# A hybrid attention block: where X's transposes, the first unit's round trip and the prelude's column sums stand

## The chip, the core and the metric

The kernel runs on one core of a Trainium2 chip. TensorE (PE) multiplies, VectorE (DVE), ScalarE (ACT) and GpSimd (POOL) work on elements, SyncE (SP) issues nearly all transfers. PE writes its results into PSUM, from where DVE and ACT fetch them. The metric is device microseconds of one execution, smaller is better.

## What is computed

One layer on 1024 tokens of width 1024. A vector c gives six modulation vectors. The normalized input, scaled and shifted by two of them, is u. From u come a softmax attention with a forget gate (8 heads of 64), an RWKV-7 time mix (8 heads of 64) and two sigmoid gates; their gated sum goes through w_o, and a gated feed-forward network with a short convolution follows.

```python
mod = silu(c) @ w_mod + b_mod                    # six parts of 1024
u = rms_norm(x, ln1_g) * (1 + scale1) + shift1
p_fox, p_rwkv, p_gate = split(u @ w_in)
o_fox  = softmax attention with forget gate (p_fox) @ fox_w_out
o_rwkv = rwkv7_time_mix(p_rwkv) @ rwkv_w_out
h = x + gate1 * ((sigmoid(p_gate[0]) * o_fox + sigmoid(p_gate[1]) * o_rwkv) @ w_o)
u2 = rms_norm(h, ln2_g) * (1 + scale2) + shift2
h = h + gate2 * ((silu(conv(u2 @ w_up_a)) * (u2 @ w_up_b)) @ w_down)
out = rms_norm(h, final_g)
```

The time mix is a recurrence over tokens; its state is updated with a decay, a rank-one removal and a rank-one addition per token.

## The kernel before

All large products run as three products of split operands (high times high, high times low, low times high). So each weight block is loaded as `raw`, copied to `hi` (ACT) and subtracted to `lo` (DVE) in `load_w`, and one column block of 128 for 1024 tokens is 48 products of 128x512, 24 for each half of the tokens.

**Prelude** (order on PE, SP, DVE and ACT as written). x is loaded in eight tiles (`xt`), squared, normalized and transposed by PE into `uf` (`turn`). The two modulation vectors come from `mod_load(i, ...)`, which loads eight weight tiles `wm`, `mod_add`, which adds them on DVE into `acc` with the weights `sc`, and `mod_sum`, in which PE sums `acc` over its 128 partitions column by column into `mps` and DVE adds the bias into `m1` (m in the trace) and forms `A1` (A). Part 1 (scale) is done first, then part 0 (shift). `warm` issues products that nobody reads. `u_steps` then goes through the eight tiles of each half of the tokens: uf is scaled and shifted, `u_hi` is a rounded copy, `u_lo` the rest. Behind each tile `low_part` issues four products into the four PSUM tiles `low`, two column blocks at a time.

**LoRA and RWKV stage.** PE's order comes from a planner, `Weave`: each chain is a Python generator that yields the time in planned nanoseconds after which it wants to go on, and until then the planner lays products of a queue of filler (q, k, r, v columns, gates) into PE's order. DVE, ACT, POOL and SP are ordered by the framework's scheduler from the program order and the dependencies. The time mix works in eight units (p, hf): four pairs of heads, two halves of the tokens, 8 chunks of 64 tokens each. `pre(k, p, hf)` prepares a unit: decays (`cum`, `el`, `en`), keys (`kr`, `bk`), queries (`ar`), products of them whose masked copies are E (four `tt` with the mask on DVE), and the inverse of a 32x32 triangular block: E goes by DMA to a scratch `sm`, back as M32, is inverted in 31 steps of two DVE operations (`t`, `E32`) and goes by DMA over `se` to TT. This is the round trip, for which `ready` is set: planned time plus 46000 in the first unit, 38500 in the others. `main(k, p, hf)` then transposes part of TT on DVE into X (two operations, one for each head), issues the products xi with X, then zi, uw, mz, and the chain of eight chunk states S; S waits on DVE for the product sp and the next products wait for S. A head normalization with y, mu and va ends the unit. The X transposes carry an order dependence on the last S issued so far (`marks["S"]`).

**Attention and later.** The gates that the units have not used as filler are woven into the attention as `rk_ps` products (`late_gate`), with their gs and gm on ACT and DVE. The attention itself is a chain per tile: lg (PE), nm (DVE), P (ACT, DVE), tp (PE), th (ACT), tl (DVE), ov (PE), o (ACT, DVE). Then come the branch products br, w_o and the feed-forward part.

Of the kernel before, what the change touches and what calls it, by code (L numbers as in the profile page):

```python
# [9 lines left out]
F32 = mybir.dt.float32  # L10
# [5 lines left out]
D = 1024  # L16
# [115 lines left out]
def hybrid_block(ctx: ExitStack, tc: tile.TileContext, a, out):  # L132
# [122 lines left out]
    def load_w(src, name, pool=None, n=1024, scale=None, tags=("whi", "wlo"), bufs=2):  # L255
# [14 lines left out]
        else:  # L270
            nc.scalar.copy(hi, raw)  # L271
# [73 lines left out]
    with ExitStack() as es:  # L345
# [66 lines left out]
        with tc.tile_pool(name="st", bufs=1) as st, tc.tile_pool(name="stp", bufs=2, space=PS) as stp, \  # L412
# [42 lines left out]
            def mod_sum(i, acc):  # L455
                for j0 in (0, 4):
                    ps = stp.tile([128, 4], F32, tag="mp", name=f"mps{i}{j0}")
                    for j in range(4):
                        c0 = (j0 + j) * 128
                        mm(ps[:, j : j + 1], acc[:, c0 : c0 + 128], ones[:, 0:1], start=True, stop=True)  # L460
                    tt(m1[:, i * 8 + j0 : i * 8 + j0 + 4], ps, V("b_mod", i * 8 + j0, 4), op=ALU.add)
                    if i == 1:
                        stt(A1[:, j0 : j0 + 4], m1[:, 8 + j0 : 12 + j0], 1.0, V("ln1_g", j0, 4), op0=ALU.add, op1=ALU.mult)
# [7 lines left out]
            def u_steps(half):  # L471

                cs = slice(half * NH, half * NH + NH)
                for kt in range(KT + 1):
                    if kt < KT:
                        x = uf[half][:, kt, :]
                        ts(x, x, A1[:, kt : kt + 1], m1[:, kt : kt + 1], op0=ALU.mult, op1=ALU.add)
                        nc.scalar.copy(u_hi[:, kt, cs], x)
# [33 lines left out]
            m = [mod_load(1, ("mw",)), None]  # L512
# [8 lines left out]
            m[1] = mod_load(0, ("xt", "mw"))  # L521
# [7 lines left out]
            nc.sync.dma_start(cst2, a["cst"][:, NC1:])  # L529
            for i in (1, 0):  # L530
# [292 lines left out]
        def main(k, p, hf):  # L823
# [9 lines left out]
            for h in range(2):  # L833
                i = nc.vector.transpose(X[B0[h], :, :], TT[B0[h], :, 0:32])
                if "S" in marks:
                    tc.add_manual_dep(i.ins, marks["S"].ins.name, NOSYNC)
# [1147 lines left out]
```

## Time and profile before

| | us |
|---|---|
| median of 3 runs | 1684.34 (1683.34 to 1690.74) |
| profiled execution | 1691.77 |
| its span, first to last instruction | 1690.0 |
| PE busy | 1645.9 |
| DVE busy | 1217.6 |
| ACT busy | 809.7 |
| POOL busy | 125.6 |

A row of a timeline gives start, duration, engine, line, operation, out<-in, count, and in brackets the idle time of the engine before it with what ended it. A row of the stretches gives the stretch and its length, then for each engine its busy time and in brackets the number of its instructions, then the granted clock of PE (1.00 is full), the share of DMA and GB/s. Products that follow each other overlap, so their step from start to start is shorter than their duration.

### The profile page before, as it was taken

The page shows a single profiled execution, that of the slowest core. Times are in us where ns is not written, and L with a number is a line of the kernel's source. Part 1 is how long each engine was busy: PE and PEld are TensorE (multiplying, and loading weights), DVE is VectorE, ACT ScalarE, POOL GpSimd, SP SyncE. Part 2 cuts the span into 40 slices and gives each one's busy share as a digit, 9 for nine tenths or more (in the row PEclk, how much of TensorE's full clock was granted, in tenths as well). Part 3 has the DMA queues.
Part 4 walks back from the last instruction along what each step waited for, and adds up shares of the span by engine and source line. Part 5 has one row for each costly group of instructions (what it writes and reads, how often), then busy time and mean ns, then how long its engine had stood idle before and what let it go on. Part 6 is the DMA issues. An engine that isn't in the chain of part 4 may idle for free.

```text
span 1690.0 us, 26279 instructions
## 1 busy us (share of the span) xinstructions
PE 1645.9 (97%) x9886; PEld 1353.3 (80%) x9886; DVE 1217.6 (72%) x2402; ACT 809.7 (48%) x1482; POOL 125.6 (7%) x150
## 2 busy tenths in 40 slices
PE   7999999999999999999999999999999999999998
PEld 7777777787877777888878888888888888888886
DVE  4786787678776625888768545897777777786677
ACT  5563334343454456667632233654444444454455
POOL 0011011111111002121022000000000000000000
PEclk9999999999999999999999999999999999999999
DMA  8487643434332226444187521133332333484463
GB/s 330 149 316 232 176 125 106 119 100 115 102 110 81 92 70 178 131 127 112 40 308 263 207 83 42 50 107 123 108 106 94 101 111 106 171 284 146 129 212 112
DMA packets 120975, 239.87 MB, mean 142 GB/s; under 512 B 39888, under 2 KB 48336, under 8 KB 120848
## 3 DMA queue, kind: packets, MB, share of 16 engines
q1 hardware_dynamic: 112896, 220.94, 40.1%
q0 software_dynamic: 7952, 17.25, 3.8%
q8 instruction: 78, 1.28, 0.3%
q14 instruction: 49, 0.40, 0.1%
HBM read 172.59 MB, written 65.54 MB: 141 GB/s over the span
## 4 chain that ended last, share of the span: by engine, by line
PE 77%; DVE 10%; DMA 6%; ACT 3%; issue 2%; SPq 2%; DVEq 0%; POOL 0%; ACTq 0%; POOLq 0%
PE X L140 13%; PE D L140 12%; PE Y L140 6%; PE wo L140 5%; PE gt L140 5%; PE ps_rkv L140 5%; PE br L140 5%; PE W L140 3%; PE rk_ps L140 3%; PE qk L140 3%; PE lg L140 2%; PE v L140 2%; PE ov L140 2%; PE sp L140 2%; PE tp L144 2%
## 5 line engine op out<-in xcount | busy, mean ns | idle before, releaser
L140 PE MATMUL D<-op,op 128*128 128x512 f32 x924 | 209.8, 389 | 0.0
L140 PEld LDWEIGHTS D<-op,op 128*128 128x128 f32 x924 | 173.3, 188 | 36.3 <-DVE op L1247 0.3
L140 PE MATMUL X<-T_m,S 128*128 128x512 f32 x440 | 107.3, 390 | 0.1
L140 PEld LDWEIGHTS X<-T_m,S 128*128 128x128 f32 x440 | 82.5, 188 | 18.2 <-ACT T_m L1672 0.6
L1246 ACT CAST op<-g 128x512 fp32r<-128x512 f32 x77 | 47.8, 621 | 72.9 <-PE D L140 48.0
L1247 DVE TENSOR_TENSOR op<-g,op 128x512 fp32r<-128x512 f32 x77 | 53.0, 689 | 41.0 <-ACT op L1246 40.8
L777 DVE TENSOR_TENSOR t<-E,M 128x60 f32<-128x60 f32 (+24 forms) x248 | 57.4, 232 | 32.6 <-DMA M<-sm 27.3
L1483 DVE SCALAR_TENSOR_TENSOR c<-ab,vec,c 128x512 f32<-128x512 f32 x88 | 65.9, 750 | 19.5 <-ACT c L1486 18.0
L273 DVE TENSOR_TENSOR lo_in<-raw_in,hi_in 128x512 fp32r<-128x512 f32 x84 | 56.5, 707 | 23.0 <-PE gt L140 12.1
L1447 DVE TENSOR_TENSOR S<-ur,S 128x512 fp32r<-128x512 f32 x66 | 45.5, 691 | 35.6 <-ACT S L1443 35.4
L1443 ACT CAST S<-ur 128x512 fp32r<-128x512 f32 x66 | 41.0, 622 | 55.6 <-DVE ur L1436 30.6
L271 ACT CAST hi_in<-raw_in 128x1024 fp32r<-128x1024 f32 x42 | 43.9, 1048 | 47.5 <-PE ps_rkv L140 18.9
L1447 DVE TENSOR_TENSOR A<-ur,A 128x512 fp32r<-128x512 f32 x64 | 44.1, 689 | 30.9 <-ACT A L1443 30.7
L140 PE MATMUL Y<-T_h,A 128*128 128x512 f32 x264 | 63.5, 389 | 0.0
L140 PE MATMUL Y<-T_h,S 128*128 128x512 f32 x264 | 63.3, 389 | 0.0
L1049 ACT ACTIVATE P<-lg,nm 128x896 f32<-128x896 f32 (+3 forms) x64 | 47.5, 743 | 30.0 <-DVE nm L1045 21.7
L140 PE MATMUL X<-B_b,A 128*128 128x512 f32 x252 | 60.8, 390 | 0.0
L140 PE MATMUL W<-B_f,A 128*128 128x512 f32 x252 | 60.6, 389 | 0.0
L140 PEld LDWEIGHTS Y<-T_h,A 128*128 128x128 f32 x264 | 49.6, 188 | 10.4
L140 PEld LDWEIGHTS Y<-T_h,S 128*128 128x128 f32 x264 | 49.6, 188 | 10.3
L779 DVE TENSOR_TENSOR E<-E,t 128x60 f32<-128x60 f32 (+24 forms) x248 | 53.2, 214 | 5.8
L1443 ACT CAST A<-ur 128x512 fp32r<-128x512 f32 x64 | 39.9, 623 | 34.2 <-PE X L140 33.6
(475 smaller groups left out, 4161.8 us busy)
## 6 DMA issues: line engine op xcount, KB each, us to landing
raw_in<-in_w_in SPq DMA_DIRECT2D x50, 512.0 KB, 3.8
wm<-in_w_mod SPq DMA_DIRECT2D x48, 512.0 KB, 7.1
ur<-in_w_up SPq DMA_DIRECT2D x44, 512.0 KB, 4.1
g<-d_g SPq DMA_DIRECT2D x35, 512.0 KB, 4.1
d_g<-gs SPq DMA_DIRECT2D x44, 256.0 KB, 2.0
d_g<-c SPq DMA_DIRECT2D x33, 256.0 KB, 4.5
d_st<-qh SPq DMA_DIRECT2D x64, 128.0 KB, 2.4
stA<-d_st POOLq DMA_DIRECT2D x8, 1024.0 KB, 6.3
```

Source lines behind the costliest of these rows:

```text
L140: nc.tensor.matmul(o, lhsT, rhs, start=start, stop=stop, skip_group_check=more)
L144: nc.tensor.transpose(o, i, eye)
L271: nc.scalar.copy(hi, raw)
L273: nc.vector.tensor_tensor(lo[:, c : c + NH], raw[:, c : c + NH], f32(hi[:, c : c + NH]), op=ALU.subtract)
L777: tt(tv, E32[:, 0:J, s : s + 1].to_broadcast([128, J, W]), M32[:, s : s + 1, s + 1 : 32].to_broadcast([128, J, W]), op=ALU.mult)
L779: tt(E32[:, 0:J, s + 1 : 32], E32[:, 0:J, s + 1 : 32], tv, op=ALU.add)
L1049: nc.scalar.activation(e[:, 0:n], lg[:, 0:n], AF.Exp, bias=nm[:, 0:1], accum_out=nm[:, 1:2])
L1246: nc.scalar.copy(hi, src)
L1247: tt(lo, src, f32(hi), op=ALU.subtract)
L1443: nc.scalar.copy(hi, src)
L1447: tt(lo, src, f32(hi), op=ALU.subtract)
L1483: stt(c, ab[:, x + hf * NH : x + hf * NH + NH], V("conv_w", 22 * x + i), c, op0=ALU.mult, op1=ALU.add)
```

## The change

In the prelude, part 1's eight column sums follow its `acc` at once and 43 warm products come behind them. DVE goes on with part 0; part 1's m and A are made behind the fifth addition of part 0. Part 0's column sums are made tile by tile in `u_steps`: columns 0, 1, 2 to 3, 4 to 7 ahead of tiles 0, 1, 2 and 4. Every second uf is scaled on ACT. The weight tiles get five buffers in place of four, and part 0's `acc` takes one of the x tiles' eight. The first copies of `load_w` come behind the last `u_hi` on ACT. In the time mix, the first unit's `ready` is 49500 in place of 46000; X's transposes are issued 2500 planned ns ahead of xi, where that is still to come, and in any case 2500 lie between them; and they are ordered behind the last mask E issued so far, besides the last S.

```diff
         else:
-            nc.scalar.copy(hi, raw)
+            i = nc.scalar.copy(hi, raw)
+            if "u" in marks:
+                tc.add_manual_dep(i.ins, marks.pop("u").ins.name, NOSYNC)
...
             def mod_load(i, tags):
-                ws = [st.tile([128, D], F32, tag=tags[kt % len(tags)], name=f"wm{i}{kt}", bufs={"mw": 4, "xt": 8}[tags[kt % len(tags)]])
-                      for kt in range(KT)]
-                for kt, w in enumerate(ws):
-                    nc.sync.dma_start(w, a["w_mod"][kt * 128 : kt * 128 + 128, i * D : i * D + D])
-                return ws, st.tile([128, D], F32, name=f"acc{i}")
+                ws = []
+                for kt in range(KT):
+                    tag = tags[kt % len(tags)]
+                    ws.append(st.tile([128, D], F32, tag=tag, name=f"wm{i}{kt}", bufs={"mw": 5, "xt": 8}[tag]))
+                    nc.sync.dma_start(ws[-1], a["w_mod"][kt * 128 : kt * 128 + 128, i * D : i * D + D])
+                return ws
...
-            def mod_sum(i, acc):
-                for j0 in (0, 4):
-                    ps = stp.tile([128, 4], F32, tag="mp", name=f"mps{i}{j0}")
-                    for j in range(4):
-                        c0 = (j0 + j) * 128
-                        mm(ps[:, j : j + 1], acc[:, c0 : c0 + 128], ones[:, 0:1], start=True, stop=True)
-                    tt(m1[:, i * 8 + j0 : i * 8 + j0 + 4], ps, V("b_mod", i * 8 + j0, 4), op=ALU.add)
-                    if i == 1:
-                        stt(A1[:, j0 : j0 + 4], m1[:, 8 + j0 : 12 + j0], 1.0, V("ln1_g", j0, 4), op0=ALU.add, op1=ALU.mult)
+            def mod_sum(i, acc, ps, j0, j1):
+                for j in range(j0, j1):
+                    mm(ps[:, j : j + 1], acc[:, j * 128 : j * 128 + 128], ones[:, 0:1], start=True, stop=True)
+
+            def mod_out(i, ps, j0, j1):
+                c = slice(i * 8 + j0, i * 8 + j1)
+                tt(m1[:, c], ps[:, j0:j1], V("b_mod", i * 8 + j0, j1 - j0), op=ALU.add)
+                if i == 1:
+                    stt(A1[:, j0:j1], m1[:, c], 1.0, V("ln1_g", j0, j1 - j0), op0=ALU.add, op1=ALU.mult)
...
                 for kt in range(KT + 1):
+                    if half == 0 and kt in (0, 1, 2, 4):
+                        ks = kt, max(kt + 1, 2 * kt)
+                        mod_sum(0, acc[0], mps[0], *ks)
+                        mod_out(0, mps[0], *ks)
                     if kt < KT:
                         x = uf[half][:, kt, :]
-                        ts(x, x, A1[:, kt : kt + 1], m1[:, kt : kt + 1], op0=ALU.mult, op1=ALU.add)
-                        nc.scalar.copy(u_hi[:, kt, cs], x)
+                        if kt % 2:
+                            nc.scalar.activation(x, x, AF.Identity, scale=A1[:, kt : kt + 1], bias=m1[:, kt : kt + 1])
+                        else:
+                            ts(x, x, A1[:, kt : kt + 1], m1[:, kt : kt + 1], op0=ALU.mult, op1=ALU.add)
+                        marks["u"] = nc.scalar.copy(u_hi[:, kt, cs], x)
...
-            m[1] = mod_load(0, ("xt", "mw"))
+            acc[0] = st.tile([128, D], F32, tag="xt", name="acc0", bufs=8)
+            ws[0] = mod_load(0, ("xt", "mw"))
...
             for i in (1, 0):
                 for kt in range(KT):
-                    mod_add(kt, *m[1 - i])
-                mod_sum(i, m[1 - i][1])
-                warm((6, 40)[i])
+                    mod_add(kt, ws[i], acc[i])
+                    if i == 0 and kt == 4:
+                        mod_out(1, mps[1], 0, KT)
+                if i == 1:
+                    mod_sum(1, acc[1], mps[1], 0, KT)
+                    warm(43)
...
-                    tt(E[:, c0 : c0 + 4, h, 0:2, :].rearrange("p c a s -> p c (a s)"), hx(ps[h], 128),
+                    marks["E"] = tt(E[:, c0 : c0 + 4, h, 0:2, :].rearrange("p c a s -> p c (a s)"), hx(ps[h], 128),
...
-            ready = weave.now + (46000 if k == 0 else 38500)
+            ready = weave.now + (49500 if k == 0 else 38500)
...
+            yield max(0, o["ready"] - weave.now - 2500)
             for h in range(2):
                 i = nc.vector.transpose(X[B0[h], :, :], TT[B0[h], :, 0:32])
-                if "S" in marks:
-                    tc.add_manual_dep(i.ins, marks["S"].ins.name, NOSYNC)
-            yield max(0, o["ready"] - weave.now)
+                for x in ("S", "E"):
+                    if x in marks:
+                        tc.add_manual_dep(i.ins, marks[x].ins.name, NOSYNC)
+            yield 2500
```

What this does to the order is shown at three places. First DVE in the prelude, from the last addition of part 0 to the sixth u tile (mps are the column sums in PSUM). Before:

```order
L453 SCALAR_TENSOR_TENSOR acc_334<-wm_325,sc,acc_334 128x1024
L461 TENSOR_TENSOR m_103<-mps_420,vec 128x4
L461 TENSOR_TENSOR m_103<-mps_426,vec 128x4
L477 TENSOR_SCALAR uf_172<-uf_172,A_102,m_103 128x512 x2
L481 TENSOR_TENSOR u_lo<-uf_172,u_hi 128x512
L477 TENSOR_SCALAR uf_172<-uf_172,A_102,m_103 128x512
```

From there u_lo and uf take turns. And now:

```order
L457 SCALAR_TENSOR_TENSOR acc_318<-wm_333,sc,acc_318 128x1024
L465 TENSOR_TENSOR m_103<-mps_350,vec 128x1
L489 TENSOR_SCALAR uf_172<-uf_172,A_102,m_103 128x512
L465 TENSOR_TENSOR m_103<-mps_350,vec 128x1
L493 TENSOR_TENSOR u_lo<-uf_172,u_hi 128x512
L465 TENSOR_TENSOR m_103<-mps_350,vec 128x2
L489 TENSOR_SCALAR uf_172<-uf_172,A_102,m_103 128x512
L493 TENSOR_TENSOR u_lo<-uf_172,u_hi 128x512 x2
L465 TENSOR_TENSOR m_103<-mps_350,vec 128x4
L489 TENSOR_SCALAR uf_172<-uf_172,A_102,m_103 128x512
L493 TENSOR_TENSOR u_lo<-uf_172,u_hi 128x512
```

The four m stand between the u tiles, and half of the uf are gone from DVE. On PE, column sums 2 to 3 stand behind the four low products of tile 0, and 4 to 7 behind those of tile 2.

Second, PE at the first unit's xi, with the engines whose semaphores a row waits for (qk_0 and qk_1 are the two halves of a column block of q or k, ssq belongs to the next unit's keys). Before:

```order
L140 MATMUL xi_0_2151<-X_0_1680,E_0_1421 32x32 [waits DVE_49,Activation_49]
L140 MATMUL xi_0_2151<-X_0_1680,E_0_1421 32x32 [waits DVE_49]
L140 MATMUL xi_0_2151<-X_0_1680,E_0_1421 32x32 x14
L140 MATMUL qk_0_2114<-u_hi,lo_in_2022 128x512
L140 MATMUL ssq_0_2135<-kp_0_2128,blk_r 128x512 [waits PE_49,Activation_49]
L140 MATMUL ssq_0_2135<-kp_0_2128,blk_r 128x512 [waits Pool_49]
L140 MATMUL qk_0_2114<-u_hi,lo_in_2022 128x512 x3
L140 MATMUL qk_1_2192<-u_hi,hi_in_2021 128x512 [waits DVE_49]
```

Now:

```order
L140 MATMUL qk_0_2107<-u_hi,lo_in_2015 128x512 x7
L140 MATMUL ssq_0_2128<-kp_0_2121,blk_r 128x512 [waits PE_49,Activation_49]
L140 MATMUL ssq_0_2128<-kp_0_2121,blk_r 128x512 [waits Pool_49]
L140 MATMUL qk_0_2107<-u_hi,lo_in_2015 128x512
L140 MATMUL qk_1_2168<-u_hi,hi_in_2014 128x512 [waits DVE_49]
L140 MATMUL qk_1_2168<-u_hi,hi_in_2014 128x512 x7
L140 MATMUL qk_1_2168<-u_lo,hi_in_2014 128x512 x3
L140 MATMUL xi_0_2180<-X_0_1675,E_0_1416 32x32 [waits PE_49]
```

xi has moved behind 17 products of 128x512, the beginning of qk_1 among them. DVE's order around this place is the same in both programs: X, two lo casts, X, v. In the later units the four masks E of the next unit stand ahead of X on DVE now, where they stood behind it.

Third, PE at the end of the attention, down to the first branch product (rk_ps are gate products). Before:

```order
L140 MATMUL ov<-tl_21_9232,vh_8675 128x256
L140 MATMUL rk_ps<-u_hi,lo_in_8734 128x512 x7
L140 MATMUL ov<-th_22_9247,vh_8675 128x256
L140 MATMUL ov<-th_22_9247,vh_8675 128x128
L140 MATMUL ov<-tl_22_9252,vh_8675 128x128
L140 MATMUL ov<-tl_22_9252,vh_8675 128x256
L140 MATMUL rk_ps<-u_hi,lo_in_8734 128x512
L140 MATMUL br_00_9340<-fx_6916,hi_br_9285 128x512
```

Now:

```order
L140 MATMUL ov<-tl_21_9232,vh_8763 128x256
L140 MATMUL ov<-th_22_9242,vh_8763 128x256
L140 MATMUL ov<-th_22_9242,vh_8763 128x128
L140 MATMUL ov<-tl_22_9248,vh_8763 128x128
L140 MATMUL ov<-tl_22_9248,vh_8763 128x256
L140 MATMUL br_00_9331<-fx_7055,hi_br_9276 128x512
```

The gate products among the last attention products are gone. Over the whole program the gates in the time mix have 528 products in place of 432, those in the attention 240 in place of 336, and the last of these stands some 40 of the 160 products ov<-th ahead of the end, where before it stood behind the last.

More of the change, by code (lines that the diff above doesn't have):

```diff
@@ L511, in hybrid_block @@
             xs = [load_x(half) for half in range(2)]
-            m = [mod_load(1, ("mw",)), None]
+            ws = {1: mod_load(1, ("mw",))}
+            acc = {1: st.tile([128, D], F32, name="acc")}
             uf = [st.tile([128, KT, NH], F32, name=f"uf{half}") for half in range(2)]
@@ L529, in hybrid_block @@
             nc.sync.dma_start(cst2, a["cst"][:, NC1:])
+            mps = [stp.tile([128, 8], F32, tag="mp", name=f"mps{i}") for i in range(2)]
             for i in (1, 0):
                 for kt in range(KT):
[L532 to L534 removed]
+                    mod_add(kt, ws[i], acc[i])
[4 more added lines that the diff above has]
+                    warm(43)
             for raw, hi, _ in low_raw:
```

## The prediction

> **What bounds the kernel now.** I read the page first, then busy time by stretches, then the timelines of TensorE (PE), VectorE (DVE) and ScalarE (ACT) where PE stops.
>
> ```profile
> span 1690.0 us, 26279 instructions
> PE 1645.9 (97%) x9886; PEld 1353.3 (80%) x9886; DVE 1217.6 (72%) x2402; ACT 809.7 (48%) x1482; POOL 125.6 (7%) x150
> ```
>
> PE is idle for 1690.0 − 1645.9 = 44.1 us of the span. The change adds almost no PE work, so it can only move these 44.1 us and the time that PE runs at half clock. The stretches (columns: stretch and its length, then busy time and count of PE, PEld, DVE, ACT, POOL, the granted clock, DMA) say where the idle time lies.
>
> ```profile
> 30.20:47.30 17.10, 13.91 (x79) 13.29 (x78) 12.69 (x17) 3.29 (x5) 0.00 (x0) 0.88 0.59 238
> 47.30:62.10 14.80, 13.25 (x49) 9.59 (x49) 13.14 (x22) 6.01 (x11) 0.00 (x0) 0.91 0.39 127
> 62.10:74.20 12.10, 12.02 (x50) 8.65 (x49) 7.65 (x15) 6.55 (x11) 2.41 (x1) 1.00 0.53 175
> 74.20:223.00 148.80, 145.30 (x757) 114.46 (x755) 110.77 (x210) 69.31 (x106) 17.45 (x24) 1.00 0.73 229
> 223.00:300.00 77.00, 72.90 (x680) 55.83 (x680) 61.55 (x186) 29.89 (x55) 7.37 (x13) 0.93 0.44 118
> 300.00:645.00 345.00, 340.69 (x3221) 273.60 (x3221) 225.68 (x654) 157.51 (x275) 42.68 (x54) 1.00 0.35 101
> 645.00:799.00 154.00, 147.18 (x902) 128.49 (x901) 127.10 (x257) 103.16 (x233) 28.44 (x35) 0.99 0.49 135
> 799.00:836.00 37.00, 36.44 (x218) 30.92 (x218) 29.26 (x63) 25.04 (x60) 3.55 (x4) 1.00 0.15 48
> 836.00:850.00 14.00, 13.07 (x84) 11.28 (x82) 8.42 (x16) 8.33 (x18) 0.00 (x0) 1.00 0.17 53
> ```
>
> The first three are the prelude, up to 645 come LoRA and RWKV units, the last three are the attention. Behind the prelude PE is full nearly everywhere, because projections and gates are woven in as filler. Their amount is fixed: what one stage takes, another lacks.
>
> **Prelude.** These rows carry the chain from the modulation sums to the first product.
>
> ```profile
> 25.05 2.71 DVE L453 SCALAR_TENSOR_TENSOR acc<-wm,sc,acc 128x1024 f32<-128x1024 f32 x2 [1.52 <-DMA wm<-in_w_mod]
> 17.20 13.05 PE L140 MATMUL tr<-xwa,xt 128*128 128x128 f32 x112 [1.04 <-ACT uf L520]
> 30.04 1.28 DVE L453 SCALAR_TENSOR_TENSOR acc<-wm,sc,acc 128x1024 f32<-128x1024 f32 x1 [2.28 <-DMA wm<-in_w_mod]
> 33.93 0.75 DVE L451 TENSOR_SCALAR acc<-wm,sc 128x1024 f32<-128x1024 f32 x1
> 34.71 9.21 DVE L453 SCALAR_TENSOR_TENSOR acc<-wm,sc,acc 128x1024 f32<-128x1024 f32 x7
> 45.13 0.16 DVE L461 TENSOR_TENSOR m<-mps,vec 128x4 f32<-128x4 f32 x1 [1.21 <-PE mps L140]
> 46.10 1.00 DVE L477 TENSOR_SCALAR uf<-uf,A,m 128x512 f32<-128x512 f32 x2
> 46.69 1.14 ACT L478 CAST u_hi<-uf 128x512 fp32r<-128x512 f32 x2 [3.02 <-DVE uf L477]
> 62.56 1.29 DVE L273 TENSOR_TENSOR lo_in<-raw_in,hi_in 128x512 fp32r<-128x512 f32 x2 [1.77 <-ACT hi_in L271]
> 68.13 0.62 ACT L478 CAST u_hi<-uf 128x512 fp32r<-128x512 f32 x1 [0.44 <-DVE uf L477]
> 74.20 2.01 PE L140 MATMUL ps_rkv<-u_hi,hi_in 128*128 128x512 f32 x8
> DMA to landing us min/median/max: 5.5/9.7/10.7
> ```
>
> The last row is the landing time of the weights wm, from the view of that tile.
>
> Gains, step by step. A fifth buffer lets the fifth weight load of the first sum start without waiting for DVE, and each load behind it one DVE operation sooner. Of the waits 1.52 + 2.28 = 3.8 I take half, 1.9, since the transfers share the same DMA engines. Between the two sums DVE loses 33.93 − 31.32 = 2.6 to two round trips through PE. In the changed order the second sum follows at once, and the first one's m and A come after its fifth operation, when PE has long delivered: two short operations of 0.16 stay, 2.3 goes. From the end of the second sum, 34.71 + 9.21 = 43.92, to u_hi at 46.69 are 2.77. With one column instead of two groups, a round trip of 1.21, m at 0.16 and uf at 0.5 are left, 1.9; a gain of 0.9. Together 5.1 at the first product.
>
> Losses. Each m behind the first now stands in DVE's queue between u tiles, and its column sum stands in PE's queue behind products that wait for u_lo. The 2-column and the 4-column m therefore each stop DVE for a round trip (1.21) and three or four products, some 2.0, and uf, u_lo and the lo casts queue behind them, and PE behind those: 2 × 2.0 = 4.0. Four uf of 0.5 in this half go to ACT, which is busy for 6.01 of 14.80 there: −2.2 with their gaps. Net loss 1.8. The cast of the next weight block that stands among the second half's u_hi (DVE waits 1.77 for it) moves behind them. PE is busy for 12.02 there with 48 products, 11.0 at 0.23 (below), so I take 0.5 of that difference. The cast itself costs nothing in its new place: from the last u_hi (68.13) to its first product (74.20) are 6 us, and ahead of it stand one cast and one activation of about 1 us each.
>
> The sum's own buffer now takes an x slot, so the seventh load of the second sum waits for an x tile that PE reads until 30.25, and the eighth and the two raw_in loads queue behind it on SP. At the median landing time it would be there at 40.0 and stop DVE by 2; at the minimum, 35.8, by nothing. The sum is −5.1 + 1.8 − 0.5 = −3.8; for this I take **−3.0**, with bounds −7 (no trips, all DMA waits gone) and 0.
>
> **First unit.** PE's and DVE's rows:
>
> ```profile
> 218.75 1.98 PE L140 MATMUL qk<-u_lo,hi_in 128*128 128x512 f32 x8
> 220.56 1.07 PE L140 MATMUL qk<-u_hi,lo_in 128*128 128x512 f32 x4
> 223.38 0.22 PE L140 MATMUL xi<-X,E 32*32 32x32 f32 x2 [1.75 <-DVE X L834]
> 224.93 1.06 PE L140 MATMUL xi<-X,E 32*32 32x32 f32 x30 [1.33 <-DVE X L834]
> 222.80 0.43 DVE L834 STREAM_TRANSPOSE X<-TT 32x256 f32<-32x256 f32 x1 [5.00 <-DMA TT<-se]
> 224.91 0.75 DVE L368 SCALAR_TENSOR_TENSOR v<-ps_rkv,omu,sh_rkv 128x512 f32<-128x512 f32 x1
> 224.00:231.00 7.00, 6.07 (x42) 4.73 (x42) 6.19 (x21) 3.58 (x7) 0.19 (x1) 0.51 0.45 133
> ```
>
> PE waits 1.75 + 1.33 = 3.08 for X, and the clock then stands at half for nearly 7 us, worth some 3.4. In the changed order xi comes 17 products later. The products put ahead of it include the next column half of qk, though, whose PSUM bank DVE frees with v, and v still stands in DVE's queue behind both X and ends at 224.91 + 0.75 = 225.66. One product takes (220.56 − 218.75)/8 = 0.23, so PE, done with the first four at 220.56 + 1.07 = 221.63, arrives there six products later, at 223.0, and waits 2.65 instead of 3.08. The wait changes its name: −0.4. Whether the clock falls after one wait of 2.65 as after two in a row, the trace doesn't show; of 3.4 I take −0.9 (0 to −3.4). **−1.3.**
>
> **Later units.** PE waits behind DVE at two larger places:
>
> ```profile
> 296.00 0.48 PE L140 MATMUL sp<-UV,E 128*64 128x64 f32 x4 [2.38 <-DVE S L899]
> 295.70:302.50 6.80, 6.50 (x41) 4.79 (x42) 5.77 (x17) 1.83 (x3) 1.26 (x1) 0.50 0.41 114
> 480.33 0.43 DVE L834 STREAM_TRANSPOSE X<-TT 32x256 f32<-32x256 f32 x1 [4.78 <-DMA TT<-se]
> 482.56 0.33 PE L144 MATMUL at<-cst,ar 128*128 128x128 f32 x1 [1.64 <-DVE E L757]
> ```
>
> At 482.56 PE waits for the masks E of the next unit, which stand on DVE behind X, and X waits 4.78 for the DMA of TT. In the changed order the masks come first, so the 1.64 go: **−1.6**. Queued behind X are then y and the copies QA, and PE needs what follows from y only at the next head sums, with gate products between, so I put nothing down for them. The other waits of X (all units have them) hold up DVE alone. At 296.00 S is late by 2.38, with a half-clock stretch worth 3.4. In the changed order the scan of cum and a pair of lo casts no longer stand between Wt and S, but bk and al do: I let half of the 2.38 and 40% of the 3.4 go, **−2.5** (0 to −5.8). That every later unit's order is dealt anew can make or remove small waits: 0, bounds ±2.5. On SP the transfers of cum, se and TT and on POOL the copies of pcd and E change places with weight loads by a row or two; PE's filler hides them, and costs of that size are in the ±2.5.
>
> **Where the filler goes.** Each unit's chain is planned 2500 ns longer, so more filler is laid into the units: two gates, 96 products, by the order. The attention runs out of gates early. 96 × 0.23 = 22 us of PE work join the units, where PE is the bound (340.69 busy of 345.00): +22. The question is what the attention gives back. It keeps 240 gate products, as many as it uses before 799 now. From there on the rows are:
>
> ```profile
> 799.00:836.00 37.00, 18.70 (x68) 12.13 (x69) 2.85 (x6) 1.00 0.15 48
> 836.00:850.00 14.00, 7.46 (x29) 4.84 (x28) 1.11 (x2) 1.00 0.17 53
> 799.00:836.00 37.00, 2.05 (x3) 7.10 (x12) 1.00 0.15 48
> 799.00:836.00 37.00, 5.80 (x20) 3.60 (x21) 1.28 (x2) 1.00 0.15 48
> 720.00:740.00 20.00, 19.07 (x126) 17.05 (x124) 18.48 (x39) 14.12 (x34) 1.90 (x3) 1.00 0.43 126
> 705.30:709.00 3.70, 3.70 (x19) 3.51 (x18) 2.59 (x6) 2.70 (x6) 0.84 (x2) 0.54 0.37 121
> ```
>
> The first two are rk_ps, the gates' products (PE, PEld, ACT). The next are the gates' gs (DVE, ACT) and lo_in (PE, PEld, DVE); then a full attention stretch. Without gates DVE has 29.26 − 2.05 − 1.28 = 25.9 in the first 37 us, and PE 36.44 − 68 × 0.23 = 20.8: DVE becomes the bound. At its best occupancy, 18.48/20 = 92%, that takes 28.0. The last 14 us are the end of the last head, a chain through PE, ACT and DVE in turn; I estimate 10.5, between DVE's 8.4 and today's 14. So 51 becomes 38.5, 12.5 back for 22: +9.5, and one half-clock stretch as at 705.30 (3.4 at half, 1.7): **+11.2**. Bounds +5 (DVE never idle: 25.9 + 8.4) and +18 (DVE at its mean of 127.10/154 = 83%, end not shortened).
>
> **Sum:** −3.0 − 1.3 − 2.5 − 1.6 + 11.2 = +2.8. The profiled execution took 1691.77, its span plus 1.8, and would take 1694.6. The median of the runs is 1684.34, 7.4 lower, and I take the same difference there: **1687.1**.
>
> **Rivals.**
>
> Slower: the tail of the attention falls to half clock. It decides from a mean clock of about 0.75 in the tail on: PE's 27 us of work (20.8 + 13.07 − 29 × 0.23 = 6.4) at two half windows in three take 27/0.67 = 40, and the longer products sit on the serial chain, so 48. The tail costs 22 − 3 = 19 and the sum is −3.0 − 5.4 + 19 = +10.6, 1694.9. For it: 296.00 shows a 2.38 wait followed by half clock. Against: 645 to 799 keeps 0.99 with small waits. The Trainium skill, "TensorE: Matmul & The Clock Gate", section "A second HAM failure mode: psum-queue depth-cycling", says that frequent micro-idles make the clock oscillate, which is this rival. The same page's "HAM oscillation — how this bites in real kernels" asks only for no idle gap above about 3.4 us; by that rule this rival cannot occur and the sum without the clock terms would be −3.0 − 0.4 − 1.2 − 1.6 + 9.5 = +3.3, but the row at 296.00 already shows half clock after a shorter gap. Chance 0.20.
>
> Stalls only change places: the −5.4 of the units come back as other waits. −3.0 + 11.2 = +8.2, 1692.5. For it: the first unit. Chance 0.15.
>
> Faster, the change does what its words say: first wait gone (−6.5), 296.00 gone (−5.8), masks (−1.6), prelude without trips (−5.6), tail bound by DVE alone (+5): −14.5, 1670. Against it stand the bank behind v and the trips. Chance 0.10.
>
> **How the numbers follow.** My forecast has 0.55, with its own range 1680 to 1694. A measurement can tell about 0.5%, 8.4 us, from no change: 1675.9 to 1692.8. Faster is the last rival less a little: 0.09. Slower: 0.17 of the clock rival, 0.05 of the stalls, 0.03 of the forecast's edge: 0.25. Same: 0.66. Leaving out most of the fast rival and the far end of the slow one, the range is 1679 to 1697.
>
> **What would show it.** The first low product 3 to 6 us earlier, then DVE idle twice before m; a PE wait of 2 to 3 us at the first unit's qk, named v, and none at xi; no wait for X ahead of the masks; attention beginning some 15 us later and ending its last 40 us with PE near 70% and DVE near 90%. The forecast is wrong if the attention shortens by over 18 us, or if its last stretch shows half clock throughout.

## The result

The changed kernel takes 1712.66 us (median of 6 runs, 1707.21 to 1713.77) beside 1683.84 (6 runs, 1682.29 to 1690.74) for the one before: 1.0152 times as long, 95% interval 1.0134 to 1.0170, estimated over all executions of both. By this ratio it is slower by some 26 us; the two medians alone lie 28.8 apart. Its time is outside the range that was given. The profiled execution took 1713.07, 0.4 above its own median; that of before had taken 1691.77, above all 23 later executions of it that were timed in one series (1683.5 to 1690.2). The spans of the two profiled executions therefore differ by 21.3 us only. All ratios are over executions in the chip's ordinary state: of the run with 49500 alone, two of twelve executions, 1807.94 and 2016.14 us at granted clocks of 0.85 and 0.75, are left out.

### The profile after

The head of the page:

```profile
span 1711.3 us, 26280 instructions
PE 1652.1 (97%) x9883; PEld 1357.8 (79%) x9883; DVE 1216.3 (71%) x2394; ACT 815.7 (48%) x1488; POOL 123.8 (7%) x148
```

Busy time by stretches, cut at the first ps_rkv, the first rk_ps and the first br product (stretch and length, then busy time and count of PE, PEld, DVE, ACT, POOL, granted clock, DMA). Before:

```profile
74.20:645.01 570.81, 558.89 (x4657) 443.89 (x4656) 398.01 (x1048) 256.70 (x435) 67.51 (x91) 0.99 0.46 137
645.01:852.17 207.16, 197.01 (x1201) 170.70 (x1200) 165.72 (x335) 138.09 (x313) 31.98 (x38) 0.99 0.41 115
```

After:

```profile
74.54:674.64 600.10, 581.67 (x4753) 460.91 (x4752) 403.00 (x1056) 268.03 (x454) 67.40 (x91) 0.99 0.45 136
674.64:873.66 199.02, 179.94 (x1105) 156.97 (x1103) 161.32 (x327) 128.08 (x293) 29.84 (x36) 0.97 0.39 109
822.00:859.70 37.70, 29.92 (x182) 26.14 (x181) 29.59 (x63) 19.54 (x48) 4.46 (x5) 0.91 0.10 27
859.70:873.66 13.96, 9.77 (x67) 8.06 (x66) 10.80 (x21) 8.37 (x18) 0.00 (x0) 0.99 0.21 71
```

The LoRA and unit stage has 96 products more (4753 against 4657) and is 29.3 us longer: 22.8 of work, and 18.4 us idle (600.10 − 581.67) in place of 11.9. The attention has the 96 products less and is only 8.1 us shorter: its busy time falls by 17.1, its idle time rises from 10.2 to 19.1. The prelude ends 0.3 later, what follows the attention takes 0.2 less. In the last 52 us of the attention neither engine is full: PE is busy for 79% and DVE for 78% of the first 37.7.

The prelude on DVE, the waits for m (in brackets the idle time ahead of the row and what ended it):

```profile
41.44 0.16 DVE L465 TENSOR_TENSOR m<-mps,vec 128x1 f32<-128x1 f32 x1 [0.48 <-PE mps L140]
45.58 0.16 DVE L465 TENSOR_TENSOR m<-mps,vec 128x2 f32<-128x2 f32 x1 [1.96 <-PE mps L140]
51.56 0.16 DVE L465 TENSOR_TENSOR m<-mps,vec 128x4 f32<-128x4 f32 x1 [3.85 <-PE mps L140]
```

and on PE around them:

```profile
42.95 0.50 PE L140 MATMUL low<-u_hi,hi_in 128*128 128x512 f32 x1 [0.92 <-ACT u_hi L490]
...
48.85 0.63 PE L140 MATMUL low<-u_lo,hi_in 128*128 128x512 f32 x1
49.28 0.63 PE L140 MATMUL low<-u_hi,hi_in 128*128 128x512 f32 x1
49.71 0.63 PE L140 MATMUL low<-u_lo,hi_in 128*128 128x512 f32 x1
50.13 1.38 PE L140 MATMUL mps<-cst,acc 128*128 128x1 f32 x8
```

The first low product comes 4.4 us earlier than before (47.36). Then DVE stops twice. The last column sums stand behind eight low products that run at half clock, 0.43 us apart and not 0.23. From the first low product to ps_rkv it takes 31.6 us where before took 26.8. Half clock costs 5.1 us of this (before 1.3) and idle time 2.7 (before 1.6), so most of what was won at the first product is lost to the clock.

The first unit on PE, and DVE at the same place:

```profile
227.71 1.83 PE L140 MATMUL qk<-u_hi,hi_in 128*128 128x512 f32 x5 [2.63 <-DVE v L370]
```

```profile
224.80 0.43 DVE L853 STREAM_TRANSPOSE X<-TT 32x256 f32<-32x256 f32 x1 [4.92 <-DMA TT<-se]
225.17 1.24 DVE L275 TENSOR_TENSOR lo_in<-raw_in,hi_in 128x512 fp32r<-128x512 f32 x2
226.44 0.44 DVE L853 STREAM_TRANSPOSE X<-TT 32x256 f32<-32x256 f32 x1
226.91 0.75 DVE L370 SCALAR_TENSOR_TENSOR v<-ps_rkv,omu,sh_rkv 128x512 f32<-128x512 f32 x1
```

The wait is named v as expected. The largest wait of PE in the units is new; PE first, then DVE from behind the last Mt to S (`...` marks rows left out):

```profile
541.38 0.39 PE L140 MATMUL gt<-u_lo,hi_in 128*128 128x512 f32 x1
545.57 0.34 PE L140 MATMUL sp<-UV,E 128*64 128x64 f32 x4 [3.81 <-DVE S L919]
```

```profile
540.78 0.74 DVE L748 SCALAR_TENSOR_TENSOR ar<-kr,nkk,el 128x512 f32<-128x512 f32 x1
541.45 0.68 DVE L752 TENSOR_TENSOR ar<-r,el 128x512 f32<-128x512 f32 x1
...
542.18 0.74 DVE L749 SCALAR_TENSOR_TENSOR kr<-kr,vec,al 128x512 f32<-128x512 f32 x1
542.85 0.68 DVE L275 TENSOR_TENSOR lo_in<-raw_in,hi_in 128x512 fp32r<-128x512 f32 x1
...
543.59 0.68 DVE L275 TENSOR_TENSOR lo_in<-raw_in,hi_in 128x512 fp32r<-128x512 f32 x1
544.19 0.68 DVE L750 TENSOR_TENSOR bk<-kr,en 128x512 f32<-128x512 f32 x1
544.79 0.53 DVE L753 TENSOR_SCALAR al<-al,vec,oka 128x512 f32<-128x512 f32 x1
545.25 0.27 DVE L919 TENSOR_SCALAR S<-sp,pcd 128x64 f32<-128x64 f32 x1
```

DVE has no idle time there. S, for which PE waits, stands in its queue behind seven long operations, five of the preparation of a later unit and two lo casts, with a few short steps of the inversion between them.

### The profile page after: what moved, and what is told of

It is laid out like the page before. It is cut to its first block, busy times and chain, and to the rows that moved or that the text cites. A ratio compares the mean times of both kernels' runs of the same rounds, so it can differ in the third digit from the quotient of the medians.

```text
span 1711.3 us, 26280 instructions
## 1 busy us (share of the span) xinstructions
PE 1652.1 (97%) x9883; PEld 1357.8 (79%) x9883; DVE 1216.3 (71%) x2394; ACT 815.7 (48%) x1488; POOL 123.8 (7%) x148
## 4 chain that ended last, share of the span: by engine, by line
PE 75%; DVE 12%; DMA 6%; ACT 4%; issue 2%; SPq 1%; POOL 0%; DVEq 0%; ACTq 0%; POOLq 0%
PE X L140 13%; PE D L140 12%; PE Y L140 6%; PE gt L140 5%; PE ps_rkv L140 5%; PE wo L140 5%; PE br L140 5%; PE W L140 3%; PE v L140 2%; PE qk L140 2%; PE sp L140 2%; PE lg L140 2%; PE rk_ps L140 2%; PE ov L140 2%; PE tr L140 2%
## 5 line engine op out<-in xcount | busy, mean ns | idle before, releaser
L275 DVE TENSOR_TENSOR lo_in<-raw_in,hi_in 128x512 fp32r<-128x512 f32 x88 | 60.2, 720 | 27.3 <-ACT hi_in L271 13.9
```

Source lines behind the costliest of these rows:

```text
L275: nc.vector.tensor_tensor(lo[:, c : c + NH], raw[:, c : c + NH], f32(hi[:, c : c + NH]), op=ALU.subtract)
```

## The experiments

Each is set against runs of before in its own series, whose medians were 1686.8 to 1688.0. Theory A at the start: the 2500 planned ns that are forced between X and xi in every unit lengthen the planned chain, filler is laid into it, and the attention then lacks it. Rival B: the order dealt anew on DVE. Rival C: the prelude. The table gives the stages of the profiled executions, for the runs that bear on the time mix: idle is length less PE busy time, half clock the time lost in the windows in which the clock record grants 0.50 (half their length). Both together are called stalls below.

| kernel | gate products in units | units: length, idle, half clock | attention: length, idle, half clock | ratio to before |
|---|---|---|---|---|
| before | 432 | 570.8, 11.9, 6.8 | 207.2, 10.2, 1.7 | 1 |
| after | 528 | 600.1, 18.4, 6.8 | 199.0, 19.1, 5.1 | 1.0152 |
| prelude alone | 432 | 574.1, 13.3, 8.5 | 205.1, 10.0, 0.0 | 1.0006 |
| time mix alone | 528 | 596.8, 14.9, 8.5 | 201.3, 17.7, 10.2 | 1.0137 |
| 2500 alone | 528 | 593.0, 12.5, 6.8 | 201.0, 17.4, 10.2 | 1.0104 |
| conditional 2500 | 432 | 565.7, 10.6, 1.7 | 205.1, 10.1, 0.0 | 0.9982 |
| gates capped | 432 | 583.2, 24.7, 7.1 | 211.6, 13.5, 3.1 | 1.0144 |
| 2500 taken off elsewhere | 432 | 568.7, 13.2, 1.7 | 207.7, 10.8, 1.7 | 1.0008 |
| 1250 forced | 480 | 572.2, 7.2, 1.7 | 202.6, 12.7, 5.1 | 1.0011 |
| 1750 forced | 528 | 588.7, 12.0, 1.7 | 202.0, 17.0, 12.0 | 1.0095 |
| no stop, 3500 | 528 | 598.6, 19.2, 6.8 | 202.0, 19.3, 8.5 | 1.0155 |
| no stop, 2500 | 480 | 588.6, 16.7, 8.5 | 201.1, 12.5, 3.7 | 1.0102 |

Each row is one execution. How far chance goes is seen where two kernels have the same order of PE in the units: before, the prelude alone and one trip alone (below) show 18.7, 21.9 and 15.9 us of stalls there, after and the time mix alone 25.3 and 23.4. So a difference of a few us between two rows of the units can't be told from chance.

**The prelude alone**: the diff without its time-mix part.

> The changed prelude with the time mix as before; gate products by the order as before, 432 in the units and 336 in the attention. Theory A (the forced 2500 planned ns per unit pull filler into the units, and the prelude only breaks even): between -2 and +2 us against before, the first ps_rkv product within 1 us of before's 74.20, and the waits of DVE at m of about 2 and 4 us there again. Rival B (the re-dealt order of DVE in the units is the loss): the same here. Rival C (the prelude, with a half-clock window behind the m, is a good part of the loss): +4 us or more.

1688.22, ratio 1.0006 (0.9995 to 1.0016). ps_rkv began at 75.42, 1.2 later than before, m waited 2.38 and 4.17 for mps. The prelude breaks even; C falls.

**The time mix alone**: before with its three edits.

> Before's prelude with all of the time mix's edits (49500, X behind the last E, X ahead of xi and 2500 between them); gate products 528 and 240. Theories A and B: nearly the whole loss, +24 to +30 us against before. Rival C: +20 or less.

1710.51, ratio 1.0137 (1.0124 to 1.0150): 23 us, nearly the whole loss, a little under what was expected.

**The forced 2500 alone**, on before:

```diff
             yield max(0, o["ready"] - weave.now)
+            yield 2500
```

> Before with one line more: 2500 planned ns behind the wait for ready, X and its dependence where they were; gate products 528 and 240 as in the changed kernel. Theory A: +16 to +26 us against before, the first rk_ps of the attention 20 to 28 us later than before's 645.01, the attention shorter by 6 to 10. Rival B: +6 or less, since E still stands behind X on DVE and the first unit is as before.

1704.36, ratio 1.0104 (1.0091 to 1.0117), 17 us. The attention began at 666.02 and was 6.2 shorter than before. One line of planned time, with X and its dependence untouched, makes two thirds of the loss. The largest wait for S is here too, so it doesn't need the dependence on E:

```profile
536.30 0.48 PE L140 MATMUL sp<-UV,E 128*64 128x64 f32 x4 [3.81 <-DVE S L900]
```

**The 2500 made conditional**, in the changed kernel:

```diff
-            yield 2500
+            yield max(0, o["ready"] - weave.now)
```

> The changed kernel with its last wait made conditional: X and xi come 2500 ns apart only where ready is still to come; gate products 432 and 336 as before. The dependence of X on the last E, the 49500 and the prelude are the changed kernel's. Theory A: the loss is nearly gone, -4 to +6 us against before. Rival B: +15 or more.

1684.25, ratio 0.9982 (0.9969 to 0.9995). The loss is gone; the dependence on E, 49500 and the prelude stay. B as the whole cause falls.

**The gates capped**, in the changed kernel:

```diff
-                if not self.loaded:
+                if not self.loaded or not self.first and len(self.queue) <= self.floor:
                     return False
...
+        weave.floor = 6
         weave.run([main_chain(), pre_chain()])
+        weave.floor = -1
```

> The changed kernel, its forced 2500 kept, but the planner lays no more than nine gates into the units: gate products 432 and 336 as before, and where it has none left its plan goes on without filler. Theory A (the loss is the 96 gate products moved out of the attention): the attention takes 194 to 196 us again, the units end within 5 us of before, the whole is -4 to +7 us against before. Rival D (the chain of each unit itself became longer by the 2500, whatever filler there is): the units still end 20 us or more later, +18 us or more.

1710.80, ratio 1.0144 (1.0129 to 1.0159). A as worded falls: with 432 gate products the loss stays. The units end 10.9 us later than before's, not the 20 of rival D, and the attention is not shorter but 4.5 longer. Part of the loss sits at the end of the units, the last 14.96 us with the cap, beside as long a stretch near their end with the conditional 2500:

```profile
641.11:656.07 14.96, 8.31 (x117) 5.69 (x118) 3.00 (x8) 4.93 (x8) 3.38 (x4) 0.86 0.05 19
```

```profile
621.08:636.04 14.96, 14.96 (x84) 12.09 (x85) 3.56 (x6) 8.94 (x14) 4.86 (x5) 1.00 0.35 102
```

The longer plan used up its gates by 641, and the end of the last unit runs bare. The profiled execution, 1704.07, was the quickest of its four. It is 24.1 us longer than the conditional kernel's: 8.7 in this end (6.65 idle, 2.0 of clock), 6.5 in the attention, where lg waits 3.25 for a DMA (stB) at 672.12 and half clock follows, and 8.8 in the units ahead of their end, where waits as in the changed kernel stand (3.67 for S at 540.81). So added chain time is paid at the end of the units where the filler lacks there, but another part comes while gates are still left.

**v ahead of X**: the conditional kernel, with X also ordered behind the last stt of v, r or k.

```diff
-            stt(dst, ps, omu[:, ti : ti + 1], sh[:, 0:NH], op0=ALU.mult, op1=ALU.add)
+            marks["v"] = stt(dst, ps, omu[:, ti : ti + 1], sh[:, 0:NH], op0=ALU.mult, op1=ALU.add)
...
-                for x in ("S", "E"):
+                for x in ("S", "E", "v"):
```

> The kernel with the conditional wait, and X ordered also behind the last v, r or k issued so far: at the first unit v stands ahead of X on DVE. If the wait of 2.80 for v at the first unit's qk and the half-clock window behind it are one stall, both go: -4 us (2.8 and half of 3.4) against the conditional wait's 1684.25. If only the place of the wait changes (xi waits for X then, X for the DMA of TT): within 1.5 us of it.

1687.25, ratio 0.9998 (0.9988 to 1.0008). The 2.80 at qk went, 1.75 came at zi (for the copy of X on ACT). In the units, 565.48 against 565.73 us: the wait changed its place. That the median is 3.0 above the conditional kernel's, which neither case had, isn't explained by the units; in the profiled executions the difference lies in the prelude, whose code is the same (ps_rkv at 75.36 against 72.66, 8.3 against 5.1 us lost to half clock).

**X behind the last E, on before**:

```diff
-                if "S" in marks:
-                    tc.add_manual_dep(i.ins, marks["S"].ins.name, NOSYNC)
+                for x in ("S", "E"):
+                    if x in marks:
+                        tc.add_manual_dep(i.ins, marks[x].ins.name, NOSYNC)
```

> Before with one thing changed: X is ordered behind the last E issued as well as the last S. Gate products as before. The 487.08 wait for E (1.4 to 1.6) goes. Theory A: -3 to +1 us against before. Rival B (the order of DVE is the loss): +4 us or more, with waits of PE for S of 2 to 4 us as in the changed kernel.

1684.94, ratio 0.9983 (0.9973 to 0.9993): a small gain, and PE's wait for E is gone.

**49500 alone**, on before:

```diff
-            ready = weave.now + (46000 if k == 0 else 38500)
+            ready = weave.now + (49500 if k == 0 else 38500)
```

> Before with the first unit's ready at 49500 in place of 46000 and nothing else. The waits of PE for X (1.9 and 1.3) turn into one for v of 2.6 to 2.8, and one half-clock window in place of two: -2 to 0 us against before.

1685.82 (the median of ten), ratio 0.9989 (0.9980 to 0.9997), as expected. PE waited 2.74 for v there, without a half-clock window.

**2500 taken off elsewhere**: the changed kernel with three shorter waits in the same chain.

```diff
-            yield 2970
+            yield 1970
...
-            yield 2400
+            yield 1650
...
-            yield 2700
+            yield 1950
```

> The changed kernel, its forced 2500 kept, but 2500 taken from three later waits of the same chain (2970 to 1970 behind uw, 2400 to 1650 ahead of the states, 2700 to 1950 ahead of va), so that a unit's chain is planned as long as before; gate products 432 and 336 again. Theory E (what costs is the planned length of the unit's chain, which the program cannot make good whether the added time is filled with gates or not): the loss is mostly gone, -4 to +6 us against before, the attention 203 to 208 us long. Rival F (the forced distance of X to xi, or the dealt order that comes with it, costs by itself): +15 or more. The shorter waits may bring PE waits of their own for Wt, S and ysq; each would show as a row.

1688.29, ratio 1.0008 (0.9997 to 1.0020). The loss is gone with the forced distance still there and the gates back at 432: it is the planned length of the chain that costs here, not X's distance to xi.

**Half the dose**: `yield 1250` for `yield 2500`.

> The changed kernel with 1250 forced in place of 2500; gate products 480 and 288, half of the shift. Theory E: half of the loss, +10 to +16 us against before. Rival F: +20 or more.

1688.24, ratio 1.0011 (1.0002 to 1.0020). Both missed. Half of the gates moved, and nearly nothing was lost: the attention's stalls rose from 11.9 to 17.8, the units' fell to 8.9, half of before's 18.7.

**1750 forced.** In the order, the fourth unit of the changed kernel has 201 filler products between xi and zi (62 with 1250): the next pair's preparation lets the planner run filler until k, r and v are done, and the chain stands. Theory H made this stop the cause, theory G the number of gates.

> The changed kernel with 1750 forced in place of 2500. By the order 528 and 240 gate products as in the changed kernel, and 225 filler products between xi and zi of the fourth unit (62 with 1250). Theory G (the number of moved gates sets the loss) and theory H (the stop of the chain at the border of two pairs sets most of it) both: +20 to +28 us against before. A loss that goes with the planned length alone would be +10 or less, by the 1.5 measured for 1250.

1703.28, ratio 1.0095 (1.0076 to 1.0114), 16 us: less than G and H had, more than the length alone would give by the run with 1250. It sits in the attention, with 29.0 us of stalls (before 11.9); the units have 13.7, less than before.

**The stop taken away, 3500 forced**, so that the gates are 528 again:

```diff
                 while got[p, hf] < 3:
-                    weave.step()
+                    yield 200
```

> The changed kernel with 3500 forced, and the preparation of the next unit waiting in steps of 200 planned ns for k, r and v while the unit's chain goes on. Gate products 528 and 240 as in the changed kernel, 14 filler products between xi and zi of the fourth unit. Theory G: +24 to +30 us against before. Theory H: +8 to +15 (the attention's idle time of about 9 and its clock remain, the units' extra waits go).

1713.83, ratio 1.0155 (1.0133 to 1.0177), 26 us. H falls, and G's range holds it.

**The stop taken away, 2500 forced:**

> The changed kernel, 2500 forced, with only the stop taken away as in the run before; gate products 480 and 288, 18 filler products between xi and zi of the fourth unit. Theories G and H: near the run with 1250, 0 to +6 us against before. If the forced distance itself costs: +15 or more.

1704.58, ratio 1.0102 (1.0085 to 1.0120). Missed by both: with 480 gates the attention's stalls are those of 1250 (16.1 against 17.8), but the units' are 25.2 against 8.9. The number is that of the third case, the forced distance, against which the run with 2500 taken off elsewhere speaks; the longest new wait, 4.63 us at one unit's xi, is for X, which waited for the DMA of TT (the row names sh_rkv, a copy of 0.10 us that DVE does right behind X). PE, then DVE:

```profile
512.38 0.28 PE L140 MATMUL xi<-X,E 32*32 32x32 f32 x2 [4.63 <-DVE sh_rkv L366]
```

```profile
511.80 0.43 DVE L853 STREAM_TRANSPOSE X<-TT 32x256 f32<-32x256 f32 x1 [3.14 <-DMA TT<-se]
```

**The prelude with one trip**: all eight column sums of part 0 and one m ahead of the first u tile, here on the conditional kernel.

```diff
-                    if half == 0 and kt in (0, 1, 2, 4):
-                        ks = kt, max(kt + 1, 2 * kt)
-                        mod_sum(0, acc[0], mps[0], *ks)
-                        mod_out(0, mps[0], *ks)
+                    if half == 0 and kt == 0:
+                        mod_sum(0, acc[0], mps[0], 0, KT)
+                        mod_out(0, mps[0], 0, KT)
```

> The kernel with the conditional wait (1684.25), and part 0's eight column sums with one m ahead of the first u tile in place of four m among the tiles. If the two later round trips of DVE (about 2 and 4 us in the changed kernel) are what the prelude's gain goes into: the first low product 1 us later than with the conditional wait (41.8), the first ps_rkv 2 to 4 us earlier (72.7), and -2 to -4 us in all. If PE's products of low are the bound there: the first ps_rkv 1 us later.

1676.94, ratio 0.9940 (0.9927 to 0.9952): faster than both kernels, and 7.3 under the conditional kernel, twice what was expected. DVE and PE there:

```profile
43.05 0.17 DVE L465 TENSOR_TENSOR m<-mps,vec 128x8 f32<-128x8 f32 x1 [2.24 <-PE mps L140]
```

```profile
44.58 0.79 PE L140 MATMUL low<-u_hi,hi_in 128*128 128x512 f32 x1 [1.56 <-ACT u_hi L488]
```

The first low product is 2.8 later than with four trips (41.82), more than expected. From there on PE has no gap over 0.15 us until ps_rkv at 69.63, where the conditional kernel had 72.66. This is 3.0 of the 7.3; the conditional kernel's profiled execution, 1679.95, was among its quickest. Over all profiled executions with four trips, ps_rkv came at 72.66 to 75.42, over the three with one trip at 68.66 to 69.83.

**One trip with before's time mix:**

> The changed prelude with one m for all eight columns ahead of the first u tile, and the time mix as before; gate products 432 and 336. If the later round trips are what the prelude's gain went into: the first ps_rkv at 69 to 71 us where before has 74.2 and the changed prelude 72.7 to 75.4, and -3 to -6 us against before, where the changed prelude alone gave +0.8. If the 7 us came from the units beside it: within 1.5 us of before.

1682.24, ratio 0.9977 (0.9963 to 0.9991), ps_rkv at 68.66, earlier still than expected. The trips were what the prelude's gain went into.

**The conditional units with before's prelude:**

> Before's prelude, with 49500, X behind the last E and X 2500 ahead of xi only where ready is still to come. Shows what the changed prelude is worth beside these units: if it breaks even, within 1.5 us of the conditional wait with the changed prelude (1684.25 against before's 1687.38), -4 to -1 us against before.

1681.20, ratio 0.9971 (0.9960 to 0.9982), a little more than expected; its interval overlaps that of the conditional kernel with the changed prelude. The two parts, −4.9 (these units) and −3.9 (one trip) by the ratios, make −8.8 of the −10.1 of the best kernel.

**That best kernel without the stops:**

> The best so far (conditional wait, one round trip in the prelude, 1676.94) with the stops at the borders of the pairs taken away; gate products 432 and 336. If the stops of some 65 products there cost something too: -2 to -5 us against 1676.94. If their filler hides them: within 1.5 us.

1685.77, ratio 0.9993 (0.9979 to 1.0008), some 9 slower, which neither case had. The units' stalls rose from 14.2 to 21.6 us: taking the stops away gained nothing, and the order dealt in their place is worse.

## Why the prediction was wrong

The result lies on the side of the first rival (slower), but beyond its 1694.9. The step that failed most is the order dealt anew in the units, put at 0 within ±2.5; second comes the return from the attention, taken as bound by DVE. By the steps of the sum, profiled execution against profiled execution (+2.8 forecast, +21.3 found):

**Where the filler goes: right in mechanism, the return a little too large.** 96 products moved, 22.8 us (22). The attention gave back 8.1, not 10.8. From the 44th last ov<-th (at 798.28 before, where the prediction's last stretches begin) to the first br it went from 53.9 to 46.2 us, 7.7 less, where 12.5 was put down: its gate products went, but PE's idle time there rose from 3.3 to 12.0 and 3.4 us went to half clock. The step took DVE as the bound at 92%; the rows show DVE at 78%, and PE waiting for one link of the attention's chain after another:

```profile
834.23 0.39 PE L140 MATMUL ov<-tl,vh 128*128 128x256 f32 x1 [1.39 <-DVE tl L1105]
840.64 0.45 PE L140 MATMUL ov<-th,vh 128*128 128x256 f32 x2 [1.75 <-DVE o L1138]
850.25 0.87 PE L144 MATMUL tp<-cst,P 128*128 128x128 f32 x3 [1.00 <-DVE nm L1074]
```

The mean clock in the first 37.7 of its last 52 us is 0.91, so the first rival's half-clock stretches came in part; with 1750 forced the attention lost 12 us to them.

**The units' stalls: wrong in sign, the largest miss.** The prediction let −5.4 go (first unit −1.3, S −2.5, masks −1.6) and put the order dealt anew at 0 with bounds ±2.5. Idle time rose by 6.5 in their place. Of the single waits, two were read rightly: v at the first unit waited 2.63 (2.65), and no wait for E is left. The 2.38 at S, of which half was to go, only split into two that come to 2.43:

```profile
301.74 0.34 PE L140 MATMUL sp<-UV,E 128*64 128x64 f32 x4 [0.84 <-DVE S L919]
305.75 0.34 PE L140 MATMUL sp<-UV,E 128*64 128x64 f32 x4 [1.59 <-DVE S L919]
```

The half-clock windows at these two places lost 3.4 us in place of 6.8. So about what was put down for the places that were priced came, and "0, ±2.5" was the mis-sized term: beyond these places new stalls of some 12 us came, 3.81 at one S, 1.32 at another, 2.9 at two v, and two more half-clock windows of 1.7 each. The two chains were dealt against each other anew, and the runs show from 8.9 to 26 us of units' stalls for small changes of the plan, and 31.8 with the cap. The rival that stalls change places was the right one here, though its 1692.5 allowed for too little. The attention began 29.6 us later, not some 15. Neither of the two things that were to show the forecast wrong came (the attention 18 us shorter, its end at half clock throughout): both look at the attention, and the largest miss is in the units.

**The prelude: −3.0 forecast, +0.3 found.** First product −4.4 (−5.1). The two trips were put at 2.0 each; they are 1.96 and 3.85, because the last one's column sums stand behind eight low products at half clock, where the sum had three or four at 0.23 each.

**From the profile to the median: 7 us.** The prediction took the same difference for both kernels. Before's profiled execution had 0.989 as its granted clock; of its 23 later executions only the slowest had as little, and the quickest, span 1681.7, had 0.995. After's profiled execution was an ordinary one, so the 7.4 that were taken off for the median are a part of the miss of their own.

Two parts of the loss are thus told apart. First, the forced 2500 alone costs 17 us: the attention's stalls rise from 11.9 to 27.6 while the units' sum hardly changes (18.7 to 19.3). The attention's stalls follow the gates that it lost: 24 to 29 us in the five kernels with 528 gate products in the units, 16 and 18 in the two with 480, 10 to 12.5 with 432 (the cap, with the wait for stB, has 16.7).

Second, the other time-mix edits add some 6 on top, of which 3.8 lie in the units by the profiled executions, no more than their scatter, though without the forced 2500 the same edits gain (0.9971). The units' stalls follow no number that was counted: with 480 gates they are 8.9 and 25.2. Why one deal of DVE is good and another bad stays open. The rows at 545.57 show how it comes about at one place. With 1750 forced, S stands ahead of bk and the casts, and PE waited 0.42 for it (0.90 for the next S, behind them); DVE, then PE:

```profile
531.49 0.75 DVE L749 SCALAR_TENSOR_TENSOR kr<-kr,vec,al 128x512 f32<-128x512 f32 x1
...
532.28 0.28 DVE L919 TENSOR_SCALAR S<-sp,pcd 128x64 f32<-128x64 f32 x1
532.48 0.68 DVE L750 TENSOR_TENSOR bk<-kr,en 128x512 f32<-128x512 f32 x1
...
533.67 1.29 DVE L275 TENSOR_TENSOR lo_in<-raw_in,hi_in 128x512 fp32r<-128x512 f32 x2
```

```profile
532.62 0.34 PE L140 MATMUL sp<-UV,E 128*64 128x64 f32 x4 [0.42 <-DVE S L919]
```

A version that pins S by itself was not tried.

## What to carry to other kernels

Filler is a fixed stock. A planned wait that is forced in each of eight units draws on it, and the stage behind gives back only what its own chain doesn't need: before adding planned time, count what the order moves and ask which chain bounds the stage that loses it. Where a scheduler deals the order anew, the old waits are a poor guide to the new ones; price the deal by a run with half the step, since it need not be linear. A result that several later steps need was better fetched here in one round trip ahead of them than piece by piece among them.

## What the hardware showed

Half-clock windows don't follow the length of the wait alone. At the first unit, the conditional kernel and the capped one have the same products on PE up to a wait of 2.80 us for the same v. With the conditional 2500 three products then took 1.65 us, and the stretch stands at half clock:

```profile
225.77 1.65 PE L140 MATMUL qk<-u_hi,hi_in 128*128 128x512 f32 x3 [2.80 <-DVE v L370]
```

```profile
225.20:228.60 3.40, 2.83 (x7) 2.25 (x8) 2.80 (x10) 1.10 (x3) 0.19 (x1) 0.50 0.58 181
```

With the gates capped, six took as long, at full clock:

```profile
226.53 1.66 PE L141 MATMUL qk<-u_hi,hi_in 128*128 128x512 f32 x6 [2.80 <-DVE v L371]
```

```profile
226.50:230.00 3.50, 3.48 (x44) 2.69 (x45) 2.89 (x12) 1.84 (x4) 0.19 (x1) 1.00 0.42 145
```

With 1250 forced, a wait of 1.54 in the attention was followed by 6.8 us at half:

```profile
830.59 0.80 PE L140 MATMUL lg<-stA 128*128 128x512 f32 x1 [1.54 <-ACT P L1069]
```

```profile
830.50:837.30 6.80, 6.71 (x23) 5.93 (x24) 5.28 (x12) 4.25 (x9) 0.00 (x0) 0.50 0.00 0
```

The Trainium skill, "TensorE: Matmul & The Clock Gate", section "HAM oscillation — how this bites in real kernels", asks only that no idle gap exceeds about 3.4 us; the half-clock stretches at the waits of 1.54 and 2.80 disagree, and the measurement decides. The windows fall differently from execution to execution: those of before went from 1683.5 to 1690.2 us, with mean clocks of 0.995 to 0.989. The stage behind the attention, where PE's order is the same in every kernel here, took from 834.0 us with 1.2 lost to half clock (no stop, 3500) to 841.0 with 9.2 (no stop, 2500).
